# The last token block's closing contraction steps in two column halves, its squares to a spare PSUM bank, its sum of squares added on VectorE, its row written by three stores

## The chip, the cores and the metric

The kernel runs on one core of a Trainium2 chip. The metric is device microseconds for one execution; three runs of the kernel before gave 817.07, 815.26 and 815.65 us, median 815.65 us. Five engines work side by side, each through its own queue in order: TensorE (PE, matmuls, and PEld for its weight loads), VectorE (DVE), ScalarE (ACT), GpSimd (POOL) and SyncE (SP, which only issues DMAs here).

## The reference, cut to what matters

One encoder layer on 512 tokens of width 1024. The change lies in the last lines of the last sub-layer:

```python
def conv_ffn(h, w_up, conv_w, conv_b, w_down):
    ...
    return (jax.nn.silu(gate) * val) @ w_down
...
h = rmsnorm(x, pre_ffn_g[l])
x = x + rmsnorm(conv_ffn(h, w_up[l], conv_w[l], conv_b[l], w_down[l]), post_ffn_g[l])
```

So for each token the down projection gives a row y of 1024 numbers, contracted over 2816 hidden features; the row is divided by the root of its mean square (plus 1e-6), multiplied by a gain, and added to the residual x, and the sum is the output.

## The kernel before, in words

The layer runs in this order: combined projection, attention and recurrent heads with the output projection, cross-attention, then the feed-forward part (up projection with convolution from line 1089, down projection from line 1185). Only the end of the last is touched.

**Tiling.** The 512 tokens are four blocks of 128 rows; the rows of an output block lie on the 128 partitions, its 1024 columns are two halves of 512 (`half(0)`, `half(1)`), and 512 float32 columns fill one PSUM bank. Every matrix product is made in three matmuls, high part by high part, high by low, low by high (`mm3`, lines 278 to 280).

**The down projection** (from line 1185) is done by seven block products instead of eight (`PRODUCTS`, line 35). Tokens are split into blocks 0, 1 and 2, 3; features into even and odd; columns into two halves. The loop of line 1201 runs the products p = 0 to 6. Each contracts over `NP` = 11 steps j of 128 features, for two blocks b, into two banks `y[0]`, `y[1]`; sums and differences of the products give the four quarters of the result. Step j uses the left operand `laid[p, j // 4]` (built by `lay_ahead` some steps earlier) as the stationary matrix and 512 columns of a weight tile as the moving one. Weight tiles come through `take()`, which loads, casts and splits them ahead of need (lines 222 and 224), in a fixed order written out in `plan`.

**The last product**, p = 6, adds into the two banks of product 0 (`y_first`). Its steps 0 to 4 are done inside the loop, both blocks in turn. The last six steps are done outside (lines 1236 to 1243): first all six for block 0, then all six for block 1, so that block 0 is finished while block 1 still multiplies. At that point the other half of each block's columns, `half(1)`, has already been treated after product 3: its square sums are in the small tile `rows[b]`, its gained product is the first entry of `parts[b]`.

**Finishing a block.** `out_part` (line 1176) takes one half of the row:

- line 1179, ScalarE: squares of `y`, written to the tile `yg` and summed per row into column i of the small tile `ss` (an activation followed by a read of the accumulator);
- lines 303 and 306, GpSimd (`rstd_part`): `ss[:, i+4]` = square sum / 1024 + what stood in `ss[:, i+3]` (for i = 0 the 1e-6), and for the last half the power -1/2 into `ss[:, 8]`;
- line 1182, VectorE: `yg` = y times gain, written over the squares.

`finish` (line 1193) then does for each part, in the order in which parts were made, line 339 on VectorE (x += yg * rstd) and a store to the output of that part's columns, issued by SP and by ScalarE's queue in turn (line 1196). For blocks 0 and 1 the parts are `half(1)`, then `half(0)`.

**Where the program waits.** Waits between engines are put in by the tile layer from what each instruction reads and writes; within an engine the layer takes, of the instructions that its own model holds ready, the one that stands first in the program. Two earlier places serve the prediction. In `strassen_pair` (line 1128), which does part of the up projection, the 512 columns of a bank `m` take two results of 256 columns: product t2 in columns 256 to 511, which VectorE reads at line 1146, and later product t1 in columns 0 to 255 (its matmuls are issued at line 1141). In `put_kv`, one bank holds keys in columns 0 to 127 and values in columns 128 to 255: VectorE reads the values at line 126, ScalarE squares the keys at line 725.

**PSUM** has eight banks, two for each of the tags b, s, c, o. The tag-b banks hold `y_first` to the end. The tag-o banks were last used by product 3 (line 1224 reads them). Temporary tiles of tag `th` have four rooms.

Of the kernel before, what the change touches and what calls it, by code (L numbers as in the profile page):

```python
# [13 lines left out]
ACT = mybir.ActivationFunctionType  # L14
ALU = mybir.AluOpType
# [4 lines left out]
D = 1024  # L20
# [12 lines left out]
NP = NF // 2  # L33
# [56 lines left out]
def layer(tc, io, out):  # L90
    nc = tc.nc
# [13 lines left out]
    def small():  # L105
        return sm.tile([P, 16], F32, name="small", tag="small")

    def bank(tag):
        return ps.tile([P, 512], F32, name="ps_" + tag, tag=tag)
# [4 lines left out]
    def tmp2(shape=(P, 512), dt=F32, tag="ta"):  # L114
        return t2.tile(list(shape), dt, name="tmp2", tag=tag, bufs=TMP_BUFS[tag])
# [13 lines left out]
    def half(c):  # L129
        return slice(c * 512, c * 512 + 512)  # L130
# [135 lines left out]
    def unit(n):  # L266
        taken[0] += 1
        issue_ahead()
        wh, wl = pending.popleft()
        return wh.rearrange("p (k n) -> p k n", k=n), wl.rearrange("p (k n) -> p k n", k=n)  # L270

    def take():
        taken[0] += 1
        issue_ahead()
        return pending.popleft()

    def mm3(o, a, b, start, stop, again=False):
        nc.tensor.matmul(o, a[0], b[0], start=start, stop=False, skip_group_check=again)  # L278
        nc.tensor.matmul(o, a[0], b[1], start=False, stop=False, skip_group_check=again)  # L279
        last_mm[0] = nc.tensor.matmul(o, a[1], b[0], start=False, stop=stop, skip_group_check=again).ins  # L280

    def blk(b):
        return slice(b * P, (b + 1) * P)
# [16 lines left out]
    R = 8  # L300

    def rstd_part(ss, i, last):
        nc.gpsimd.tensor_scalar(ss[:, i + 4:i + 5], ss[:, i:i + 1], 1.0 / D, ss[:, i + 3:i + 4] if i else EPS,
                                op0=ALU.mult, op1=ALU.add)
        if last:
            last_pow[0] = nc.gpsimd.tensor_tensor(out=ss[:, R:R + 1], in0=ss[:, i + 4:i + 5], in1=nhalf[:, 0:1],
                                                  op=ALU.pow).ins
# [29 lines left out]
    def residual_add(ss, part, xb):  # L337
        yg, cols = part
        nc.vector.scalar_tensor_tensor(out=xb[:, cols], in0=yg, scalar=ss[:, R:R + 1], in1=xb[:, cols],
                                       op0=ALU.mult, op1=ALU.add)  # L340
# [100 lines left out]
    nhalf = const.tile([P, 16], F32, name="nhalf")  # L441
# [50 lines left out]
    ws = []  # L492
    for j in range(4):
# [4 lines left out]
        for k in range(2):  # L498
            parts = [(split_x, 2 * j + k), (split_w, wh[:, half(k)], wl[:, half(k)], w_raw[j][:, half(k)])]
# [528 lines left out]
    acts, sides, gates, last_act = [], [], {}, [None]  # L1028
    half_t = [slice(0, 256), slice(256, 512)]
# [30 lines left out]
    laid = {}  # L1060
# [30 lines left out]
    ws = [unit(8) for _ in first]  # L1091
    us = [bank(up_tags[n]) for n in range(4)]
    for part in range(2):
        cols = slice(part * 256, part * 256 + 256)
# [29 lines left out]
    def next_bank():  # L1124
        tag_at[0] += 1
        return bank(up_tags[(tag_at[0] - 1) % 4])
# [32 lines left out]
    for i in range(2, NF):  # L1159
        if i in UP_S:  # L1160
            strassen_pair(i)
        else:
            for c in range(2):
                o = next_bank()
# [11 lines left out]
    def out_part(ss, y, i, cols, last, tag="ta"):  # L1176
        n = cols.stop - cols.start
        yg = tmp2(tag=tag)[:, :n]
        nc.scalar.activation(yg, y, ACT.Square, accum_out=ss[:, i:i + 1])
        rstd_part(ss, i, last)  # L1180
        g0 = cols.start % 512
        nc.vector.tensor_mul(yg, y, acts[2][cols.start // 512][:, 3, g0:g0 + n])
        return yg, cols
# [4 lines left out]
    def products(y, p, j, w, b):  # L1188
        hi, lo = laid[p, j // 4]
        ac, wc = (slice(None), j % 4, blk(b)), half(j % 2)  # L1190
        mm3(y[b], (hi[ac], lo[ac]), (w[0][:, wc], w[1][:, wc]), j == 0 and p < 6, j == NP - 1, p == 6)

    def finish(b, ss, done):
        for i, part in enumerate(done):
            residual_add(ss, part, x[b])
            (nc.sync, nc.scalar)[i % 2].dma_start(out[blk(b), part[1]], x[b][:, part[1]])

    rows = [small() for _ in range(NB)]
    parts = [[] for _ in range(NB)]
    last = NP - 6  # L1200
    for p, (_, tag) in enumerate(PRODUCTS):
        y = [bank(tag) for _ in range(2)] if p < 6 else y_first
# [33 lines left out]
    ws = {}  # L1236
    for j in range(last, NP):
        ws[j] = take() if j % 2 == 0 else ws.get(j - 1, w)
    for b in range(2):
        for j in range(last, NP):  # L1240
            products(y, 6, j, ws[j], b)
        parts[b].append(out_part(rows[b], y[b], 1, half(0), True, "th"))
        finish(b, rows[b], parts[b])
    assert taken[0] == N_UNITS
    ctx.close()

# [100 lines left out]
```

## Time and profile before

| what | value |
|---|---|
| runs | 815.26, 815.65, 817.07 us, median 815.65 |
| profiled execution, from its first to its last instruction | 813.8 us (the page gives no other time of this execution) |
| median less that span | 1.85 us |
| PE busy | 803.3 us, 99% of the span |
| last matmul starts | 806.60 us |
| last VectorE instruction (line 339) ends | 810.16 us |
| last store is issued | 810.18 us |
| span ends | 813.8 us |

In a timeline row the columns are: start in us from the span's start, duration, engine, line, operation, output tile from input tiles, shape, count, and in brackets how long the engine was idle before and what ended that. In a row of groups the columns are: line, engine, operation, tiles, shapes and count, then the busy time in us and the mean of one in ns, then the idle time before. A "q" behind an engine's name (SPq, ACTq) is its queue issuing a DMA or waiting for a semaphore.

### The profile page before, as it was taken

The page shows a single profiled execution, that of the slowest core. Times are in us where ns is not written, and L with a number is a line of the kernel's source. Part 1 is how long each engine was busy: PE and PEld are TensorE (multiplying, and loading weights), DVE is VectorE, ACT ScalarE, POOL GpSimd, SP SyncE. Part 2 cuts the span into 40 slices and gives each one's busy share as a digit, 9 for nine tenths or more (in the row PEclk, how much of TensorE's full clock was granted, in tenths as well). Part 3 has the DMA queues.
Part 4 walks back from the last instruction along what each step waited for, and adds up shares of the span by engine and source line. Part 5 has one row for each costly group of instructions (what it writes and reads, how often), then busy time and mean ns, then how long its engine had stood idle before and what let it go on. Part 6 is the DMA issues. An engine that isn't in the chain of part 4 may idle for free.

```text
span 813.8 us, 11771 instructions
## 1 busy us (share of the span) xinstructions
PE 803.3 (99%) x4426; PEld 691.0 (85%) x4426; DVE 574.7 (71%) x868; ACT 482.1 (59%) x796; POOL 136.9 (17%) x213
## 2 busy tenths in 40 slices
PE   9999999999999999999999999999999999999996
PEld 7888888889998887888888898899999998888885
DVE  5456587469886865855453767987777788888765
ACT  5675757459988874644543553665555545566651
POOL 0111201053233102301010311211111111000301
PEclk9999999999999999999999999999999999999999
DMA  8685645569899753256634158776665677278852
GB/s 296 202 259 139 160 103 117 118 159 247 229 250 254 182 172 126 78 181 157 180 117 142 33 164 208 154 200 166 179 171 143 150 200 178 91 208 278 239 130 104
DMA packets 42457, 139.61 MB, mean 172 GB/s; under 512 B 5280, under 2 KB 6560, under 8 KB 42400
## 3 DMA queue, kind: packets, MB, share of 16 engines
q1 hardware_dynamic: 28944, 97.43, 35.5%
q0 software_dynamic: 12160, 38.54, 26.2%
q10 hardware_dynamic: 1296, 2.89, 1.0%
q8 instruction: 34, 0.56, 0.3%
q14 instruction: 23, 0.19, 0.1%
HBM read 135.17 MB, written 25.17 MB: 197 GB/s over the span
## 4 chain that ended last, share of the span: by engine, by line
PE 92%; DVE 3%; ACT 2%; issue 1%; POOL 1%; DMA 0%; DVEq 0%; POOLq 0%; SPq 0%; ACTq 0%
PE ps_b L279 10%; PE ps_b L280 10%; PE ps_b L278 10%; PE ps_s L278 6%; PE ps_s L280 6%; PE ps_s L279 6%; PE ps_o L278 5%; PE ps_o L279 5%; PE ps_o L280 5%; PE ps_c L278 5%; PE ps_c L280 5%; PE ps_c L279 5%; PE ps_c L647 3%; PE ps_o L893 2%; PE ps_s L872 2%; PE ps_o L882 2%
## 5 line engine op out<-in xcount | busy, mean ns | idle before, releaser
L222 ACT CAST wh<-raw 128x1024 fp32r<-128x1024 f32 x110 | 113.7, 1035 | 114.6 <-PE ps_b L279 35.3
L224 DVE TENSOR_TENSOR wl<-raw,wh 128x1024 fp32r<-128x1024 f32 (+1 forms) x77 | 92.3, 1201 | 72.2 <-ACT wh L222 72.0
L278 PE MATMUL ps_b<-big,wh 128*128 128x512 f32 (+1 forms) x344 | 122.3, 355 | 0.0
L280 PE MATMUL ps_b<-big,wl 128*128 128x512 f32 (+1 forms) x344 | 121.2, 352 | 0.0
L279 PE MATMUL ps_b<-big,wh 128*128 128x512 f32 (+1 forms) x344 | 121.2, 352 | 0.0
L280 PEld LDWEIGHTS ps_b<-big,wl 128*128 128x128 f32 x344 | 65.1, 189 | 8.5 <-DMA wl<-in_wu_dram 0.2
L278 PEld LDWEIGHTS ps_b<-big,wh 128*128 128x128 f32 x344 | 65.1, 189 | 8.3
L279 PEld LDWEIGHTS ps_b<-big,wh 128*128 128x128 f32 x344 | 65.1, 189 | 8.1
L673 DVE TENSOR_TENSOR big<-big 128x512 f32<-128x512 f32 x64 | 47.2, 755 | 9.6 <-PE ps_c L647 4.0
L278 PE MATMUL ps_s<-wh,big 128*128 128x512 f32 (+1 forms) x140 | 53.4, 383 | 0.0
L279 PE MATMUL ps_s<-wl,big 128*128 128x512 f32 (+1 forms) x140 | 53.3, 381 | 0.0
L280 PE MATMUL ps_s<-wh,big 128*128 128x512 f32 (+1 forms) x140 | 53.0, 379 | 0.0
L230 POOL DMA_DIRECT2D wl<-in_w_dram x33 | 29.3, 887 | 126.7 <-ACT wl L229 91.5
L122 DVE TENSOR_TENSOR big<-ps_o,big 128x512 fp32r<-128x512 f32 x54 | 36.9, 687 | 15.0 <-ACT big L121 13.4
L121 ACT CAST big<-ps_o 128x512 fp32r<-128x512 f32 x54 | 31.7, 588 | 18.5 <-PE ps_o L996 7.5
L278 PE MATMUL ps_s<-big,wh 128*128 128x256 f32 (+1 forms) x120 | 40.0, 334 | 0.0
L279 PE MATMUL ps_s<-big,wh 128*128 128x256 f32 (+1 forms) x120 | 40.0, 333 | 0.0
L280 PE MATMUL ps_s<-big,wl 128*128 128x256 f32 (+1 forms) x120 | 40.0, 333 | 0.0
L278 PE MATMUL ps_o<-wh,big 128*128 128x512 f32 (+1 forms) x102 | 39.2, 385 | 0.0
L279 PE MATMUL ps_c<-big,wh 128*128 128x256 f32 (+1 forms) x120 | 39.1, 326 | 0.0
L278 PE MATMUL ps_c<-big,wh 128*128 128x256 f32 (+1 forms) x120 | 39.1, 326 | 0.0
L280 PE MATMUL ps_c<-big,wl 128*128 128x256 f32 (+1 forms) x120 | 39.1, 326 | 0.0
(315 smaller groups left out, 2149.3 us busy)
## 6 DMA issues: line engine op xcount, KB each, us to landing
raw<-in_w_dram SPq DMA_DIRECT2D x91, 512.0 KB, 3.6
wl<-in_w_dram POOLq DMA_DIRECT2D x33, 512.0 KB, 7.3
sum_t<-in_wd_dram SPq DMA_DIRECT2D x20, 512.0 KB, 6.3
tmp<-in_wu_dram SPq DMA_DIRECT2D x14, 512.0 KB, 6.9
sum_t<-in_wd_dram POOLq DMA_DIRECT2D x10, 512.0 KB, 8.4
sum_t<-sum_t POOLq DMA_DIRECT2D x10, 512.0 KB, 7.5
big<-sum_t SPq DMA_DIRECT2D x10, 512.0 KB, 4.7
raw<-sum_t SPq DMA_DIRECT2D x10, 512.0 KB, 4.4
```

The costliest lines, as they stand in the source:

```text
L121: nc.scalar.copy(hi, src)
L122: (eng or nc.vector).tensor_sub(lo, src, hi.bitcast(F32))
L222: nc.scalar.copy(wh, raw)
L224: last_low[0] = nc.vector.tensor_sub(wl[:, :by_dma], raw[:, :by_dma], wh[:, :by_dma].bitcast(F32)).ins
L230: nc.gpsimd.dma_start(wl[:, by_dma:], source(i)[:, by_dma:], accum_op=ALU.add)
L278: nc.tensor.matmul(o, a[0], b[0], start=start, stop=False, skip_group_check=again)
L279: nc.tensor.matmul(o, a[0], b[1], start=False, stop=False, skip_group_check=again)
L280: last_mm[0] = nc.tensor.matmul(o, a[1], b[0], start=False, stop=stop, skip_group_check=again).ins
L647: nc.tensor.matmul(o[:, b, :], kc[:, blk(b)], qc[:, blk(b)] if m == 1 else pat(qk, b * P, [[2 * m, P // (2 * m)], [T + m, 2], [1, m]]), st ...
L673: nc.vector.tensor_tensor(out=c, in0=c, in1=pat(tt, toff + off, [[2, npair], [gap, 2], [0, m]]), op=ALU.mult)
L872: nc.tensor.matmul(s, qT[h // 4][:, h % 4, blk(qb)], kT[:, 2 * (h // 4) + c, :], start=c == 0, stop=c == 1)
L882: nc.tensor.transpose(o[:, c, :], e[:, 0, blk(c)], ident)
```

## The change

Block 0 is as before. For block 1 the six closing steps become four full ones and then, for each half of the 512 columns (`half_t`: 0 to 255, 256 to 511), the last two steps on 256 columns. After each half ScalarE squares its 256 columns with a scale of 1/32, so that the square sum is already divided by 1024; the squares go to a fresh bank of tag o, not to `yg`. VectorE multiplies the 256 columns by the gain into a tile of its own, and adds the half's square sum to what is there already (one column). After both halves GpSimd only takes the power, in one instruction in place of two. `finish` now has three parts: columns 512 to 1023, 0 to 255 and 256 to 511, with three instructions of line 339 and three stores (SP, ScalarE's queue, SP).

```diff
-    for b in range(2):
-        for j in range(last, NP):
-            products(y, 6, j, ws[j], b)
-        parts[b].append(out_part(rows[b], y[b], 1, half(0), True, "th"))
-        finish(b, rows[b], parts[b])
+    for j in range(last, NP):
+        products(y, 6, j, ws[j], 0)
+    parts[0].append(out_part(rows[0], y[0], 1, half(0), True, "th"))
+    finish(0, rows[0], parts[0])
+    for j in range(last, NP - 2):
+        products(y, 6, j, ws[j], 1)
+    ss = rows[1]
+    for c, cols in enumerate(half_t):
+        for j in range(NP - 2, NP):
+            hi, lo = laid[6, j // 4]
+            wc = slice(j % 2 * 512 + cols.start, j % 2 * 512 + cols.stop)
+            mm3(y[1][:, cols], (hi[:, j % 4, blk(1)], lo[:, j % 4, blk(1)]), (ws[j][0][:, wc], ws[j][1][:, wc]),
+                False, j == NP - 1, True)
+        nc.scalar.activation(bank("o")[:, cols], y[1][:, cols], ACT.Square, scale=D ** -0.5, accum_out=ss[:, 1 + c:2 + c])
+        yg = tmp2(tag="th")[:, :256]
+        nc.vector.tensor_mul(yg, y[1][:, cols], acts[2][0][:, 3, cols])
+        nc.vector.tensor_scalar(ss[:, 5 + c:6 + c], ss[:, 1 + c:2 + c], ss[:, 4 + c:5 + c], None, op0=ALU.add)
+        parts[1].append((yg, cols))
+    nc.gpsimd.tensor_tensor(out=ss[:, R:R + 1], in0=ss[:, 6:7], in1=nhalf[:, 0:1], op=ALU.pow)
+    finish(1, ss, parts[1])
```

## The prediction

> **What bounds the kernel now.** I read the page first. TensorE fills the span, and its clock is never held back while it works:
>
> ```profile
> span 813.8 us, 11771 instructions
> PE 803.3 (99%) x4426; PEld 691.0 (85%) x4426; DVE 574.7 (71%) x868; ACT 482.1 (59%) x796; POOL 136.9 (17%) x213
> ...
> PEclk9999999999999999999999999999999999999999
> ...
> PE 92%; DVE 3%; ACT 2%; issue 1%; POOL 1%; DMA 0%; DVEq 0%; POOLq 0%; SPq 0%; ACTq 0%
> ```
>
> The change touches only the last 11 us, so what counts is the chain after the last matmul. The timeline of the end shows it (start, duration, engine, line):
>
> ```profile
> 802.74 0.39 PE L278 MATMUL ps_b<-wh,big 128*128 128x512 f32 x1
> ...
> 804.65 1.42 DVE L339 SCALAR_TENSOR_TENSOR big<-tmp,small,big 128x512 f32<-128x512 f32 x2 [0.30 <-POOL small L306]
> ...
> 806.10 0.34 ACTq L1196 DMA_DIRECT2D out_dram<-big  x1
> ...
> 806.60 0.39 PE L280 MATMUL ps_b<-wh,big 128*128 128x512 f32 x1
> 807.02 0.60 ACT L1179 ACTIVATE tmp<-ps_b 128x512 f32<-128x512 f32 x1 [3.39 <-PE ps_b L280]
> 807.51 0.19 ACT L1179 ACTIVATION_READ_ACCUMULATOR tmp<-ps_b 128x1 f32 x1
> 807.74 0.69 DVE L1182 TENSOR_TENSOR tmp<-ps_b,big 128x512 f32<-128x512 f32 x1 [1.67 <-ACT tmp L1179]
> 807.81 0.26 POOL L303 TENSOR_SCALAR small<-small 128x1 f32<-128x1 f32 x1 [3.19 <-ACT tmp L1179]
> 808.16 0.54 POOL L306 TENSOR_TENSOR small<-small,nhalf 128x1 f32<-128x1 f32 x1
> 808.74 1.42 DVE L339 SCALAR_TENSOR_TENSOR big<-tmp,small,big 128x512 f32<-128x512 f32 x2 [0.30 <-POOL small L306]
> 809.52 0.33 SPq L1196 DMA_DIRECT2D out_dram<-big  x1
> 810.18 0.34 ACTq L1196 DMA_DIRECT2D out_dram<-big  x1
> ```
>
> Block 1's eighteen closing matmuls start at 802.74 and the last at 806.60, so the pitch at 512 columns is 3.86/17 = 0.227 us. ScalarE squares from 807.02 and has the sum at 807.70. GpSimd's two instructions take until 808.70. VectorE's product (807.74 to 808.43) lies beside them and costs nothing. Line 339 runs from 808.74 to 810.16, and the stores follow. The product starts 0.04 us after ScalarE is through, although it reads only `y` and the gain. Two reasons fit: the squares were written to the product's own target, or both instructions read one bank.
>
> The stores' data, in 40 slices of 0.075 us from 809.40:
>
> ```profile
> DMA  0000000000004897999996999999998300000000
> ...
> out_dram<-big SPq DMA_DIRECT2D x1, 256.0 KB, 2.0
> out_dram<-big ACTq DMA_DIRECT2D x1, 256.0 KB, 2.0
> ```
>
> They move from 810.34 to about 811.75 without a gap: 1.41 us for both, starting 0.82 us after SP issued the first. The later one lands 2.0 us after 810.18, at 812.18; the remaining 1.6 us to 813.8 is the program's end.
>
> **The change part by part.** Block 0 and the first twelve matmuls of block 1 stay, so the halves start at 802.74 + 12 x 0.227 = 805.46. *Matmuls.* Six of 512 columns become twelve of 256. The up projection has that size:
>
> ```profile
> 555.26 0.28 PE L279 MATMUL ps_s<-big,wh 128*128 128x256 f32 x1
> 555.38 0.28 PE L280 MATMUL ps_s<-big,wl 128*128 128x256 f32 x1
> ...
> 555.70 0.37 ACT L1144 COPY tmp<-ps_s 128x256 f32<-128x256 f32 x1 [0.36 <-PE ps_s L280]
> ```
>
> The pitch is 0.12 us, and ScalarE starts 0.32 us after the last one's start. Twelve take 1.44 us where six took 1.36: 0.08 more. The first half's last matmul starts at 805.46 + 5 x 0.12 = 806.06, and its square could start at 806.38; ScalarE's queue is issuing block 0's store until 806.44, so I take 806.46.
>
> *Does the second half run beside the first half's square and product?* This decides the sign. Both halves lie in one bank. No row of before shows a matmul writing a bank while another engine reads it, so the trace has no price for that overlap. The program of before says how such pairs are ordered: in `strassen_pair` the first matmul of t1 (columns 0 to 255 of its bank) carries a wait for exactly the count that VectorE sets with line 1146, which reads columns 256 to 511 of that bank; in `put_kv` ScalarE's line 725 (columns 0 to 127) waits for exactly VectorE's line 126 (columns 128 to 255). Neither pair shares a number. So the tile layer orders by bank, reads against reads too. In the change three waits follow: the first half's product after its square, the second half's first matmul after that product, the second half's product after its square. Moving the squares to another bank frees the product's target but not the bank that both read.
>
> The Trainium skill (PSUM — Partial Sum Buffer, section "PSUM bank collisions raise a hardware error") says that two engines must not touch one bank in the same 32 partitions at once, whatever the columns, reads included, and that such pairs must be ordered. By that rule the sum is the one below; without it, rival A's. No run here shows an unordered pair.
>
> *Square of 256 columns and product.* Rows for their sizes:
>
> ```profile
> L1179 ACT ACTIVATE tmp<-ps_b 128x512 f32<-128x512 f32 x2 | 1.2, 598 | 8.6 <-PE ps_b L280 8.6
> L691 ACT ACTIVATE tmp<-ps_c 128x128 f32<-128x128 f32 x16 | 4.2, 277 | 4.3 <-PE ps_c L687 4.3
> L1146 DVE TENSOR_TENSOR tmp<-ps_s,tmp 128x256 f32<-128x256 f32 x2 | 0.8, 418 | 0.0
> L1155 DVE TENSOR_TENSOR ps_s<-ps_s,tmp 128x256 f32<-128x256 f32 x2 | 0.8, 424 | 0.0
> L854 DVE RECIPROCAL small<-small 128x1 f32<-128x1 f32 x32 | 5.0, 156 | 0.8 <-ACT tmp L853 0.6
> L523 DVE TENSOR_SCALAR tmp<-ident,rx 128x128 f32<-128x128 f32 x4 | 0.9, 282 | 5.9 <-POOL rx L297 5.9
> L339 DVE SCALAR_TENSOR_TENSOR big<-tmp,small,big 128x512 f32<-128x512 f32 x24 | 17.0, 749 | 3.5 <-POOL small L306 3.5
> L697 DVE SCALAR_TENSOR_TENSOR tmp<-ps_c,small,big 128x128 f32<-128x128 f32 x16 | 4.6, 344 | 18.1 <-POOL small L297 18.1
> ```
>
> Between 128 columns (0.277) and 512 (0.598) a square of 256 takes 0.384 us. The accumulator read starts 0.11 before its end and takes 0.19 (rows at 807.02 and 807.51): 0.465 in all. ScalarE writing PSUM is in no row; VectorE pays 6 ns for it (L1155 against L1146), and I take the same 0 with ±0.03 each. First half: square 806.46 to 806.925; product from 806.965, 0.418, to 807.38.
>
> *The stall on TensorE.* How it resumes after VectorE:
>
> ```profile
> 397.49 0.69 DVE L122 TENSOR_TENSOR big<-ps_o,big 128x512 fp32r<-128x512 f32 x1 [0.36 <-ACT big L121]
> ...
> 398.24 0.50 PE L278 MATMUL ps_o<-big 128*128 128x512 f32 x1
> ...
> 398.57 0.39 PE L279 MATMUL ps_o<-big 128*128 128x512 f32 x1
> ```
>
> It resumes 0.06 after VectorE's end (398.18 to 398.24), and the next matmul comes 0.33 later, 0.10 over the pitch. So the second half starts at 807.44, its second matmul at 807.66, its sixth at 808.14, and its square at 808.46, where the whole square began at 807.02 before: 1.44 late. Queued behind the waiting matmul is nothing but its own five; the last square waits for them.
>
> *The sum.* The second square ends at 808.925. VectorE takes the product first (808.965) and the one-column sum behind it. A sum of 128x1 lies between the reciprocal's 0.156 and the 0.28 of 128 columns; I take 0.17, as it has one column, and 0.345 for the product's pitch (instructions of line 339 overlap by 0.08: two of 0.749 take 1.42). It ends at 809.48. Before, GpSimd began 0.11 after ScalarE; now the product stands in the way, and TensorE no longer covers it: 0.345 us. *GpSimd* loses line 303 (0.26 and a gap of 0.09). It follows VectorE by 0.09:
>
> ```profile
> 198.60 0.26 DVE L727 TENSOR_REDUCE small<-tmp 128x2 f32<-128x128 f32 x1
> ...
> 198.95 0.19 POOL L296 TENSOR_SCALAR small<-small 128x2 f32<-128x2 f32 x1 [2.74 <-DVE small L727]
> ...
> 795.18 0.86 POOL L306 TENSOR_TENSOR small<-small,nhalf 128x1 f32<-128x1 f32 x1
> ```
>
> Power from 809.57, 0.54, to 810.11; line 339 from 810.15 where it was 808.74: **1.41 late**. (The power took 0.86 once, in the last row, with other work about; at the end of before it took 0.54.)
>
> *Three instructions of line 339.* Between 0.344 (128 columns) and 0.749 (512) one of 256 takes 0.48. Starts 810.15, 810.82, 811.22; end 811.70, where it was 810.16: 1.54 late.
>
> *Three stores.* SP issues at 810.93 (1.41 late), ScalarE at 811.32, SP again at 811.72, its queue long free. Data can flow from 811.75. The amount is the same 512 KB, so at the old rate it ends at 813.16; the third store alone could end no sooner than 811.72 + 0.82 + 0.36 = 812.90. So 813.16 stands, 1.41 late, and with it the end.
>
> *At nothing:* the tag-o banks were last read at product 3, and both are free; the fifth `th` tile takes the room that line 339 leaves at 805.4, 3.5 us before it is written.
>
> Against the profiled execution: 813.8 + 1.41 = 815.2 us of span. The median of the runs lies 1.85 above that span, so the forecast is 815.65 + 1.41 = **817.1 us**, 0.17% slower. About 0.2% (1.63 us) is what a measurement of this kernel can tell from no change, so "no change" by that measure, though close to its edge.
>
> **The rivals.** *A, the halves do overlap:* no wait by bank. The second half's last matmul starts at 806.78, its square at 807.10, the product beside it; sum to 807.78, power to 808.41, line 339 at 808.45, 0.29 early, and the stores with it: 815.4 us. For it speaks that this is the only way in which column halves hide anything; against it, the two waits quoted above. 6 in 100.
>
> *B, the short rows of the last two stores (slower).* They are 1 KB on each of 128 partitions, where all stores before are 2 KB. Two stores of 2 KB rows give 16 rows to each of 16 DMA engines in 1.41 us: 0.088 us a row. If 1 KB costs as much, 24 rows take 2.12 us, 0.71 more: 817.8 us. It makes the kernel measurably slower as soon as a 1 KB row costs over (1.63 - 8 x 0.088)/16 = 0.058 us, against 0.044 in proportion. Against it speaks
>
> ```profile
> raw<-in_wd_dram SPq DMA_DIRECT2D x8, 512.0 KB, 3.6
> ...
> raw<-in_wd_dram SPq DMA_DIRECT2D x2, 256.0 KB, 2.6
> ```
>
> where halving the row from 4 to 2 KB saved 1.0 us, at least in proportion. The Trainium skill (DMA: Bandwidth & Descriptors, "Specifications") puts the line rate at 512 B and up, by which B would not occur; no run here shows 1 KB rows. 18 in 100.
>
> *C, VectorE's sum placed ahead of its product.* The layer could order so, as both wait for the same square. The last chain would lose 0.345, the first product would come 0.09 later: line 339 1.16 late, 816.8 us. 8 in 100.
>
> *D, a slow power at the end* (0.86, as at 795.18): 0.32 more, 817.4 us. 12 in 100.
>
> **How the numbers follow.** The forecast has 56 in 100. Runs of before lie from 815.26 to 817.07, so a median can be off by some tenths; of the forecast's 56 I give 38 to within 0.2% and 18 to slower. A gives 2 faster and 4 same; B 17 slower and 1 same; C 8 same; D 9 slower and 3 same. Together faster 0.02, same 0.54, slower 0.44. The range: downward, the squares in PSUM (2 x 0.03), ScalarE's store (0.08) and the third store's own bound (0.26) take the sum to 1.0, and a median 0.4 lower gives 816.2. Upward, B gives 817.8; with the one-column sum at 0.28 (0.11), and waits that need a queue instruction of their own (0.2 for all), 818.1. That leaves A and the tails out, under 2 in 10.
>
> **What would show it.** Right: TensorE idle for about 1.1 us between the halves (806.34 to 807.44), ended by VectorE's first product; each product starting 0.04 after ScalarE's accumulator read; the one-column sum behind the second product; line 339 starting 2.7 us after the second half's first matmul (810.15 less 807.44); no gap in the stores' data. Wrong: matmuls of the second half at a pitch of 0.12 straight behind the first (A); data of the stores taking over 1.6 us (B); the sum ahead of the product (C); a power over 0.6 us (D).

## The result, and the profile after

Fifteen runs of each kernel: 817.46 us after (816.94 to 819.32), 816.14 us before (815.16 to 817.30). The ratio is 1.0016 with a 95% interval of 1.0009 to 1.0023: the changed kernel is slower by about 1.3 us, and the point lies within the 0.2% that was called "no change". The forecast was 817.1 us, 0.17% slower, counted from the 815.65 us of the first three runs. In fifteen runs the kernel before came out 0.49 us higher, so the differences are what compares: 1.41 us forecast, 1.32 measured.

The end of the changed kernel, from its timeline (start, duration, engine, line). Lines 1252, 1254 and 1255 are the new square, product and one-column sum, line 1257 the power:

```profile
803.22 0.39 PE L278 MATMUL ps_b<-wh,big 128*128 128x512 f32 x1
...
805.94 0.28 PE L278 MATMUL ps_b<-wh,big 128*128 128x256 f32 x1
...
806.54 0.28 PE L280 MATMUL ps_b<-wh,big 128*128 128x256 f32 x1
806.59 0.34 ACTq L1196 DMA_DIRECT2D out_dram<-big  x1
806.97 0.37 ACT L1252 ACTIVATE ps_o<-ps_b 128x256 f32<-128x256 f32 x1 [2.86 <-PE ps_b L280]
807.25 0.19 ACT L1252 ACTIVATION_READ_ACCUMULATOR ps_o<-ps_b 128x1 f32 x1
807.48 0.42 DVE L1254 TENSOR_TENSOR tmp<-ps_b,big 128x256 f32<-128x256 f32 x1 [0.92 <-ACT ps_o L1252]
807.82 0.21 DVE L1255 TENSOR_SCALAR small<-small 128x1 f32<-128x1 f32 x1
807.96 0.39 PE L278 MATMUL ps_b<-wh,big 128*128 128x256 f32 x1 [1.14 <-DVE tmp L1254]
808.18 0.28 PE L279 MATMUL ps_b<-wl,big 128*128 128x256 f32 x1
...
808.65 0.28 PE L280 MATMUL ps_b<-wh,big 128*128 128x256 f32 x1
808.97 0.37 ACT L1252 ACTIVATE ps_o<-ps_b 128x256 f32<-128x256 f32 x1 [1.52 <-PE ps_b L280]
809.25 0.19 ACT L1252 ACTIVATION_READ_ACCUMULATOR ps_o<-ps_b 128x1 f32 x1
809.48 0.42 DVE L1254 TENSOR_TENSOR tmp<-ps_b,big 128x256 f32<-128x256 f32 x1 [1.45 <-ACT ps_o L1252]
809.82 0.20 DVE L1255 TENSOR_SCALAR small<-small 128x1 f32<-128x1 f32 x1
810.10 0.54 POOL L1257 TENSOR_TENSOR small<-small,nhalf 128x1 f32<-128x1 f32 x1 [5.00 <-DVE small L1255]
810.68 1.54 DVE L339 SCALAR_TENSOR_TENSOR big<-tmp,small,big 128x512 f32<-128x512 f32 x3 [0.66 <-POOL small L1257]
```

Read it from the row at 807.96. Its bracket says that TensorE sat idle for 1.14 us and that VectorE's product ended that. The last row of the first half starts at 806.54 and lasts 0.28, to 806.82; between there and 807.96 lie the first square and the first product, one behind the other, while TensorE has six matmuls left and does none of them. TensorE starts again 0.06 after the product's end (807.90) and before the one-column sum ends (808.03), so it isn't the sum or its small tile that held it. The halves do not overlap at all. The second thing to see is the chain at the bottom: the second product (809.48) stands between ScalarE's sum (809.44) and VectorE's (809.82), and GpSimd starts only at 810.10.

The stores' data in slices of 0.125 us from 809.40, changed kernel:

```profile
DMA  0000000000000000000000079999999999820000
...
out_dram<-big SPq DMA_DIRECT2D x1, 256.0 KB, 2.0
out_dram<-big ACTq DMA_DIRECT2D x1, 128.0 KB, 2.1
out_dram<-big SPq DMA_DIRECT2D x1, 128.0 KB, 2.1
```

They run from about 812.33 to 813.80, 1.47 us without a gap, where the two stores of before took 1.41.

**One clock for all profiles.** The program ahead of the closing steps is the same in all kernels but e1, yet the first of block 1's closing matmuls starts at 802.74 in the profile of before and at 803.22 in this one; in the experiments it lies between 802.63 and 804.27. That is the scatter of the runs, and it hides a change of this size. So all that follows is counted from that matmul, in us. The last column takes the span from the trace to 0.01 us (813.84 and 815.80), where the page prints one decimal; so it can differ by 0.05 from what the expectations say (11.06 for the kernel before):

| kernel | its start in the span | line 339 starts | line 339 ends | span ends |
|---|---|---|---|---|
| before | 802.74 | 6.00 | 7.42 | 11.09 |
| changed | 803.22 | 7.46 | 9.00 | 12.58 |
| e1, own banks | 803.25 | 6.28 | 7.82 | 11.39 |
| e2, squares to a free bank | 803.41 | 5.99 | 7.41 | 11.11 |
| e3, sum behind the product | 804.01 | 6.46 | 7.88 | 11.58 |
| e4, sum ahead of it | 802.63 | 5.87 | 7.28 | 10.97 |
| e5, late squares | 802.88 | 7.03 | 8.57 | 12.14 |
| e6, changed, sum ahead | 804.27 | 7.23 | 8.77 | 12.35 |
| e7, quarters | 802.79 | 5.87 | 7.55 | 10.98 |
| e8, three stores | 803.20 | 5.99 | 7.53 | 11.11 |

By this clock the change costs 12.58 - 11.09 = 1.49 us; the runs say 1.32, with the interval 0.7 to 1.9. The clock repeats well: before, e2 and e8 have the same chain up to line 339 and reach it at 6.00, 5.99 and 5.99, while their starts differ by 0.67. Of e1, e2, e3, e5, e6 and e8 there is one execution each, the profiled one, so they are compared by this clock alone; e4 and e7 were run eleven times.

### The profile page after: what moved, and what is told of

It reads as the page before. It is cut to its first block, busy times and chain, and to the rows that moved or that the text cites. A ratio compares the mean times of both kernels' runs of the same rounds, so it can differ in the third digit from the quotient of the medians.

```text
span 815.8 us, 11791 instructions
## 1 busy us (share of the span) xinstructions
PE 803.9 (99%) x4432; PEld 691.2 (85%) x4432; DVE 575.2 (71%) x872; ACT 482.5 (59%) x798; POOL 137.7 (17%) x212
## 4 chain that ended last, share of the span: by engine, by line
PE 94%; DVE 2%; DMA 1%; ACT 1%; issue 1%; SPq 0%; POOL 0%; POOLq 0%; DVEq 0%
PE ps_b L279 10%; PE ps_b L278 10%; PE ps_b L280 10%; PE ps_s L280 7%; PE ps_s L279 7%; PE ps_s L278 7%; PE ps_o L278 5%; PE ps_o L279 5%; PE ps_o L280 5%; PE ps_c L278 5%; PE ps_c L280 5%; PE ps_c L279 5%; PE ps_c L647 3%; PE ps_o L893 2%; PE ps_s L872 2%; PE ps_o L882 2%
## 5 line engine op out<-in xcount | busy, mean ns | idle before, releaser
L278 PE MATMUL ps_b<-wh,big 128*128 128x512 f32 (+1 forms) x94 | 37.8, 403 | 1.5 <-DVE tmp L1254 1.1
```

## The experiments

The theory: the tile layer puts engines that touch one PSUM bank one behind the other, whichever columns they touch and even where both only read, and so the halves cannot overlap. The rivals: the wait has another cause (the small tile, the product's room); or the tail is slow for other reasons (the sum's place, the short rows of the stores).

**e1, a bank of its own for the second half.** In products 0 and 6 block 1's columns 256 to 511 go to a bank of tag o (products 3 to 5 change their tags to make room):

```diff
+    far_bank = bank("o")
...
+        if p in (0, 6) and b == 1:
+            for t, cols in zip((y[1], far_bank), half_t):
+                wc = slice(j % 2 * 512 + cols.start, j % 2 * 512 + cols.stop)
+                mm3(t[:, cols], (hi[ac], lo[ac]), (w[0][:, wc], w[1][:, wc]), j == 0 and p < 6, j == NP - 1, p == 6)
+            return
...
+        yc = (y[1], far_bank)[c]
-            mm3(y[1][:, cols], (hi[:, j % 4, blk(1)], lo[:, j % 4, blk(1)]), (ws[j][0][:, wc], ws[j][1][:, wc]),
+            mm3(yc[:, cols], (hi[:, j % 4, blk(1)], lo[:, j % 4, blk(1)]), (ws[j][0][:, wc], ws[j][1][:, wc]),
```

> Times are counted from the start of block 1's closing steps (its first matmul of steps 5 to 10): in the changed kernel TensorE idles 1.14 us between the halves, line 339 starts at 7.46 and ends at 9.00, the span ends at 12.58; before, 6.00, 7.42 and 11.06. Here the second half of block 1's columns has a bank of its own in products 0 and 6, all else as changed (products 0 and 6 of block 1 are issued in 256 columns throughout, which costs some 0.04 us a step before the close). Theory (the second half's matmuls wait because the first half's square and product read their bank): no idle between the halves, the second half's matmuls at a pitch of 0.12 straight on, line 339 about 1.3 earlier than in the changed kernel, counted from the first matmul of the last two steps. Rival (the wait comes from something else, such as the small sum tile or the room of the product's target): idle of about 1.1 stays.

Its timeline:

```profile
806.73 0.28 PE L280 MATMUL ps_b<-wh,big 128*128 128x256 f32 x1
806.85 0.28 PE L278 MATMUL ps_o<-wh,big 128*128 128x256 f32 x1
806.97 0.28 PE L279 MATMUL ps_o<-wl,big 128*128 128x256 f32 x1
807.05 0.37 ACT L1260 ACTIVATE ps_o<-ps_b 128x256 f32<-128x256 f32 x1 [2.90 <-PE ps_b L280]
...
807.45 0.28 PE L280 MATMUL ps_o<-wh,big 128*128 128x256 f32 x1
...
809.53 1.54 DVE L339 SCALAR_TENSOR_TENSOR big<-tmp,small,big 128x512 f32<-128x512 f32 x3 [0.66 <-POOL small L1265]
```

TensorE goes on at 0.12 us from one half to the next, while ScalarE squares the first. Line 339 starts 3.40 after the first matmul of the last two steps (806.13), where the changed kernel needs 4.74 (805.94 to 810.68): 1.34 earlier, 1.3 expected. So the idle time went with the shared bank. The overlap is paid for in advance, though: block 1's products 0 and 6 run in 256 columns throughout, and even without that e1's 3.40 is no better than the 3.28 of before (6.00 less 2.72). Its second product still stands ahead of the sum. With the sum ahead one would expect about 3.06 (an estimate: 3.40 less the product's pitch of 0.34). But e1's matmuls of 256 columns cost 0.16 over the four closing steps ahead of these (803.25 to 806.13, against 2.72), and at the same 0.04 a step some 0.6 over the sixteen steps of products 0 and 6 before the close. No run joins the two, so whether that would pay is not shown.

**e2, only the squares to a free bank** (one part of the change, in the kernel before):

```diff
+    nc.scalar.activation(bank("o"), y[1], ACT.Square, accum_out=ss[:, 1:2])
+    rstd_part(ss, 1, True)
+    nc.vector.tensor_mul(yg, y[1], g)
```

> The kernel before with one part of the change: block 1's squares go to a free bank instead of the product's target, nothing else. Theory (both read one bank): the product still starts 0.04 us after ScalarE's accumulator read, about 0.72 after the square's start, and line 339 stays at 6.00 from the start of the closing steps. Rival (only the shared target held the product): the product starts within 0.1 of the square's start; line 339 at 6.00 too, as the product is not on the path.

```profile
807.69 0.58 ACT L1246 ACTIVATE ps_o<-ps_b 128x512 f32<-128x512 f32 x1 [3.39 <-PE ps_b L280]
808.18 0.19 ACT L1246 ACTIVATION_READ_ACCUMULATOR ps_o<-ps_b 128x1 f32 x1
808.41 0.69 DVE L1248 TENSOR_TENSOR tmp<-ps_b,big 128x512 f32<-128x512 f32 x1 [1.68 <-ACT ps_o L1246]
```

The product starts 0.72 after the square and 0.04 after the accumulator read, as when both had one target. Two readers of one bank are ordered, with no other target or source in common. The square takes 0.58 into PSUM, where it took 0.60 into the product's tile. Line 339 stays at 5.99.

**e5, both halves' matmuls first, then the squares and products** (the loop over the halves cut in two):

```diff
     for c, cols in enumerate(half_t):
...
                 False, j == NP - 1, True)
+    for c, cols in enumerate(half_t):
         nc.scalar.activation(bank("o")[:, cols], y[1][:, cols], ACT.Square, scale=D ** -0.5, accum_out=ss[:, 1 + c:2 + c])
```

> The changed kernel with the squares, products and sums of both halves moved behind all twelve matmuls; their order among themselves is kept. Theory (any two engines on one bank are ordered, reads among themselves too): no idle on TensorE; square, product, square, product one behind the other; line 339 at about 7.05 from the start of the closing steps. Rival (only writes are ordered against reads): the second square straight behind the first, line 339 at about 6.5. If the stall were not the matter: 7.46 as in the changed kernel.

```profile
806.91 0.28 PE L280 MATMUL ps_b<-wh,big 128*128 128x256 f32 x1
807.23 0.37 ACT L1253 ACTIVATE ps_o<-ps_b 128x256 f32<-128x256 f32 x1 [3.46 <-PE ps_b L280]
807.51 0.20 ACT L1253 ACTIVATION_READ_ACCUMULATOR ps_o<-ps_b 128x1 f32 x1
807.74 0.42 DVE L1255 TENSOR_TENSOR tmp<-ps_b,big 128x256 f32<-128x256 f32 x1 [1.53 <-ACT ps_o L1253]
808.08 0.20 DVE L1256 TENSOR_SCALAR small<-small 128x1 f32<-128x1 f32 x1
808.20 0.37 ACT L1253 ACTIVATE ps_o<-ps_b 128x256 f32<-128x256 f32 x1 [0.49 <-DVE tmp L1255]
```

The last row decides: ScalarE, which needs nothing that VectorE makes, waits 0.49 us for VectorE's product on the other columns. It starts 0.04 after that product's end (808.16) and before the one-column sum behind it ends (808.28), so it isn't the small tile that holds it. Line 339 starts at 7.03 (7.05 expected; 6.5 if reads were free). Without the stall the kernel is still 1.03 later than before at this point: two squares and two products one behind the other cost most of what the stall did.

**e6, the changed kernel with the sum ahead of the product** (rival C of the prediction, made by hand):

```diff
+        nc.vector.tensor_scalar(ss[:, 5 + c:6 + c], ss[:, 1 + c:2 + c], ss[:, 4 + c:5 + c], None, op0=ALU.add)
         yg = tmp2(tag="th")[:, :256]
         nc.vector.tensor_mul(yg, y[1][:, cols], acts[2][0][:, 3, cols])
-        nc.vector.tensor_scalar(ss[:, 5 + c:6 + c], ss[:, 1 + c:2 + c], ss[:, 4 + c:5 + c], None, op0=ALU.add)
```

> The changed kernel with VectorE's one-column sum put ahead of its product in both halves. Theory (the second product stands in the way of the sum for 0.345 us, the first sum would hold the first product for 0.13): line 339 at about 7.25 from the start of the closing steps, 0.21 earlier than changed; TensorE idle about 1.27. Rival (the sum's place does not matter, as GpSimd's start is set by ScalarE): 7.46.

Line 339 starts at 7.23 and TensorE idles for 1.26 us. The sum behind the product costs 0.23 net (0.21 expected): the prediction's 0.345, less what the first sum holds up the first product.

**e3 and e4, the sum by VectorE at full width,** behind the product and ahead of it, in the kernel before. The diff is e3's; in e4 the product is the last of the four lines:

```diff
+    nc.scalar.activation(bank("o"), y[1], ACT.Square, scale=D ** -0.5, accum_out=ss[:, 1:2])
+    nc.vector.tensor_mul(yg, y[1], g)
+    nc.vector.tensor_scalar(ss[:, 5:6], ss[:, 1:2], ss[:, 4:5], None, op0=ALU.add)
+    nc.gpsimd.tensor_tensor(out=ss[:, R:R + 1], in0=ss[:, 5:6], in1=nhalf[:, 0:1], op=ALU.pow)
```

> The kernel before, no halves, but block 1's squares scaled and in a free bank and its sum by VectorE behind the product (512 columns). Theory: the product stands between ScalarE's sum and VectorE's: 0.04 + 0.61 + 0.20, then 0.08, the power 0.54 and 0.04, 1.51 us from the accumulator read's end to line 339 where it was 1.04; line 339 at 6.47 from the start of the closing steps (before 6.00). Rival (the sum's place is free, since GpSimd loses an instruction): 5.9 or less.

> The same as the run before this one, with the sum ahead of the product. Theory: 0.04 + 0.20 + 0.08 + 0.54 + 0.04 = 0.90 us from the accumulator read's end to line 339, at 5.86 from the start of the closing steps, 0.14 earlier than before; the time 0.14 us (0.02%) lower, less than the runs can tell. Rival (VectorE's sum buys nothing over GpSimd's): 6.00.

The end of e3, then that of e4:

```profile
809.00 0.69 DVE L1247 TENSOR_TENSOR tmp<-ps_b,big 128x512 f32<-128x512 f32 x1 [1.68 <-ACT ps_o L1246]
809.61 0.20 DVE L1248 TENSOR_SCALAR small<-small 128x1 f32<-128x1 f32 x1
809.90 0.54 POOL L1249 TENSOR_TENSOR small<-small,nhalf 128x1 f32<-128x1 f32 x1 [4.01 <-DVE small L1248]
```

```profile
807.63 0.21 DVE L1247 TENSOR_SCALAR small<-small 128x1 f32<-128x1 f32 x1 [1.67 <-ACT ps_o L1246]
807.76 0.68 DVE L1249 TENSOR_TENSOR tmp<-ps_b,big 128x512 f32<-128x512 f32 x1
807.92 0.54 POOL L1248 TENSOR_TENSOR small<-small,nhalf 128x1 f32<-128x1 f32 x1 [3.42 <-DVE small L1247]
```

In e3 GpSimd starts 0.09 after a sum that had to queue behind 0.69 us of product: line 339 at 6.46, 0.46 late. In e4 the product runs beside the power: 5.87, 0.13 early. The same four instructions, in another order, make 0.59 us of difference. In the runs e4's 0.13 us can't be seen: 816.18 us (11 runs) against 815.73 (21), ratio 1.0003, 0.9995 to 1.0012.

**e7, the sum ahead, and line 339 and the stores in four pieces of 256 columns.**

```diff
+    parts[1] = [(yg0[:, t], slice(c0.start + t.start, c0.start + t.stop)) for yg0, c0 in parts[1] + [(yg, half(0))] for t in half_t]
     finish(1, ss, parts[1])
```

> The sum ahead of the product at full width, and block 1's line 339 and stores in four pieces of 256 columns in place of two of 512. Theory: line 339 at 5.86 from the start of the closing steps, in pieces 0.40 apart, ended at 7.54 (before 7.42); the first store issued 0.41 earlier than before, and the last piece, 128 KB issued at 7.57, ends its data at 8.75 where they ended at 9.01: the span's end about 0.26 earlier than before, 0.03%, within what the runs can tell. Rival (short rows cost as much as long ones): the data take 2.8 us and end over 1 us later.

**e8, only the three stores,** in the kernel before: the last part is cut in two 256-column parts ahead of `finish`.

```diff
+        if b == 1:
+            yg, _ = parts[b].pop()
+            parts[b] += [(yg[:, t], t) for t in half_t]
         finish(b, rows[b], parts[b])
```

> The kernel before with one part of the change: block 1's last 512 columns added and stored in two pieces of 256, so three stores in place of two. Theory (rows of 1 KB cost nearly in proportion): line 339 at 6.00 from the start of the closing steps and ended at 7.54 (before 7.42), the stores' data 1.41 to 1.47 us long as before, the span's end within 0.1 of 11.06. Rival B (1 KB rows cost as much as 2 KB): data 2.1 us long, the end 0.7 later.

The data of e7, then of e8, in slices of 0.125 us from 809.40:

```profile
DMA  0000079979999989981000000000000000000000
...
DMA packets 576, 0.52 MB, mean 105 GB/s; under 512 B 64, under 2 KB 576, under 8 KB 576
```

```profile
DMA  0000000000079999998998920000000000000000
...
DMA packets 432, 0.52 MB, mean 105 GB/s; under 512 B 48, under 2 KB 304, under 8 KB 432
```

e8 ends at 11.11, 0.02 after the kernel before: the third store and the third instruction of line 339 cost next to nothing where only two stores have short rows, and their data take about 1.47 us, not B's 2.1. But e7 missed its forecast: data start 0.4 earlier as expected and end at 8.9 in place of 8.75, because four stores of 1 KB rows take about 1.66 us for the amount that 2 KB rows move in 1.41. That is 1.66/32 = 0.052 us for each 1 KB row, not 0.044, but not all of it is the rows' own. By the packets' times in the traces a 1 KB row keeps its DMA engine busy for 0.047 us on average in e7 (0.046 in the changed kernel, 0.044 in e8), where a 2 KB row of before takes 0.085. So the rows cost about a tenth more for the same amount, and the rest of the stretch is gaps; the four stores are issued 0.40 us apart. The gain at the end of the span is 0.11 in place of 0.26, and the runs tell nothing: 816.18 us, ratio 1.0004, 0.9995 to 1.0013. No version was found that beats the kernel before by more than the runs can tell.

## Why the prediction was right

**The waits by bank.** Read from the waits of the program before, not from a row of its trace; the changed kernel shows all three (idle ended by line 1254; each product 0.04 after the accumulator read), e1 takes TensorE's wait away with the shared bank, e2 shows a product that waits for its square without a shared target, and e5 a square that waits for a product on other columns. The Trainium skill (PSUM — Partial Sum Buffer, section "PSUM bank collisions raise a hardware error") asks that such accesses be kept apart, and in the ends of the traces shown here they are. What the chip would do to an unordered pair wasn't tried, as that would be a race; nor do these runs tell an order by PSUM bank from one by whole PSUM tile, since every bank here is one tile. Tiles in SBUF (the on-chip memory that holds the residual x) are not ordered so: in e7 the last piece of line 339 writes its columns of x from 809.86 to 810.34, while the store of the first piece, from the same tile, was issued at 809.18 and landed 1.8 us later.

**The stall.** 4.70 us forecast from the close's start to the second half's first matmul (807.44 less 802.74), 4.74 measured; idle 1.14 against 1.1.

**The second square, the product ahead of the sum, the power.** Line 339 was forecast 1.41 late and is 1.46 late. The difference is in small terms. The first square began 0.03 late, because ScalarE took 0.04 after its store was issued where the forecast left 0.02; TensorE's restart itself was the forecast 0.06. And the one-column sum took 0.20 where 0.17 was taken. The square of 256 columns, estimated between 128 and 512, was 0.37 and 0.19 with an overlap of 0.09, 0.47 in all against 0.465. The power was 0.54, so rival D didn't occur.

**The stores.** Forecast to move as fast as before and end 1.41 late; they take 1.47 and the span ends 1.49 late. The term that was a little too small is the price of a 1 KB row: in the changed kernel itself (1.47 - 8 x 0.088)/16 = 0.048, between the 0.044 in proportion and the 0.058 from which rival B would have made the kernel measurably slower. The Trainium skill (DMA: Bandwidth & Descriptors, "Specifications") has full rate from 512 B up; here rows of 1 KB fell short of rows of 2 KB, by about a tenth in the packets' own times in e7 (0.047 against 0.085 us) and by about 15% in the whole stretch (1.66 against 1.41).

**Rival A** (overlap, 815.4 us) is refuted by the row at 807.96. **Rival C** was not the order taken; made by hand (e6) it gave 0.23 us, at line 339 and at the span's end.

**The chances.** The measured ratio, 1.0016, lies where the forecast put it, and its interval reaches over 1.002. That the two outcomes were given nearly even chances fits what the runs could settle.

## What to carry to other kernels

Splitting a result to hide its evacuation behind its own last matmuls needs, with this tile layer, parts in different PSUM banks; in one bank the matmuls of the second part wait for every reader of the first, and the readers for each other. Different banks took the wait away (e1), though no kernel here came out ahead by it. A step taken from one engine and given to another stands in that engine's queue, and its place there decides: here the same sum was worth 0.13 us ahead of a product and cost 0.46 behind it. And where a change is worth a microsecond in 800, count it from the last event that both programs share; the start of that event scattered by 1.6 us between profiles.

## What the runs showed that was not expected

Rows of 1 KB took 0.044 to 0.047 us on a DMA engine by their packets' times, where half a 2 KB row takes 0.042. Finer stores start sooner but move about 15% slower, and in e7 0.11 us of an expected 0.26 was left. ScalarE's square of 512 columns took 0.58 us into PSUM where it took 0.60 us into the product's tile.
